# One shift of the SBUF layout: all operands of TensorE's products at equal addresses modulo 512 bytes

## The chip, the core and the metric

The kernel runs on one core of a Trainium2 chip. The metric is device time in microseconds of one execution. Three runs of the kernel before gave a median of 2284.33 us (2283.15 to 2285.94). The profile was taken in a separate execution.

## What is computed

One decoder block for a sequence of 2048 tokens with 1024 channels, all in float32. Cut to what matters here:

```python
h = rmsnorm(x, g_mix_pre) * (1.0 + scale_m) + shift_m       # scale, shift, gate from c @ w_cond
q, k, v, u = split(h @ w_in)                                # 8 heads of 64, and 512 pooling channels
z = einsum('bhqd,bhkd->bhqk', qb, kb) * inv_sqrt            # stick-breaking attention
log1m = where(mask, -softplus(z), 0.0)
after = cumsum(log1m, reverse=True) - log1m
w = where(mask, exp(log_sigmoid(z) + after), 0.0)
attn = einsum('bhqk,bhkd->bhqd', w, vb)
pool = pooling_mixer(u, w_pool, pool_scale)
x = x + gate_m * rmsnorm(concat([attn, pool]) @ w_out, g_mix_post)
h = rmsnorm(x, g_ffn_pre) * (1.0 + scale_f) + shift_f
f = (silu(h @ w_gate) * (h @ w_up)) @ w_down                # 1024 -> 2816 -> 1024
x = x + gate_f * rmsnorm(f, g_ffn_post)
```

## The kernel before

**Products.** Nearly every float32 operand is kept as a high part and a low part of type float32r, made by `split` (L55 to L60: a cast on ScalarE, a subtraction on VectorE or GpSimd). A product is then three matmuls, high by high, high by low and low by high (`mm3`, L64 to L71). `nc.tensor.matmul(ps, l, r)` loads `l` (128 columns, 512 bytes a partition) into the array and streams `r` (512 columns, 2048 bytes a partition) through it. In the profile the streamed operand stands first behind the arrow and the loaded one second: `b_g<-b22h,g_s_h` streams `b22h` past the loaded `g_s_h`. The load of the next matmul's operand (engine PEld) runs while the matmul before it streams.

**Stages**, by time from the start of the profiled execution:

| stage | us | what TensorE does |
|---|---|---|
| conditioning, first projections | 0 to 75 | sums for the modulation, transposes of the rows, first products |
| projections | 75 to 286 | q, k, u for the first half of the tokens (`pieces`), then v for all (`v_pieces`) |
| attention | 286 to 836 | per head and block: z (L828, L829), transposes of the weights (L863), values (L878, L879); between them q, k, u of the second half as filling (`pieces` again, L69 to L71) |
| output projection | 810 to 1008 | `mix_products`, transposes of the new rows (L125) |
| FFN, first half of the tokens | 1008 to 1646 | gate and up (to 1431), then down |
| FFN, second half | 1646 to 2284 | gate and up (to 2064), then down |

The FFN uses a seven-product scheme on half matrices. Its token operands `b11`, `b21`, `t2`, `t3`, `t1`, `t4`, `b22` are made by `new_ops` (L1046). In gate and up they are streamed, and a weight part made by `operand` (L1041) is loaded. In down, `add_block` (L1345) loads columns of the gated rows (`g0p`, `g1p`) and streams a part of `w_down` (`w0p`, `w1p`); both come from `operand`.

**Where tiles lie.** Pools stack up from the left end of a partition or down from the right end. A tile starts at a multiple of 32 bytes; a pool's tags follow each other in the order of their first use. The left side begins with `const` (`ident` at 128 modulo 512, `mhalf`, `sumsq`, `af`, `bf`), then `c1` (`ones`, `ones_r`, small columns), `wst`, `up`, and later `att`, `qk`, or `ring` and the FFN's operands, which follow directly behind `const`. Each `operand` pair has five buffers in `ring` on the left; every sixth call takes its pair from `fx` on the right instead (L1043). The `b22` of the first half lies on the right (`opsr`, L1644), that of the second half on the left (`ops1`, L1592). The addresses that the program gives to TensorE's operands, modulo 512 bytes:

| stage | streamed | loaded |
|---|---|---|
| q, k, u products | 480 | 480 (224 for the one chunk named `fourth`) |
| v products | 224 | 480 |
| z (L828, L829) | `kt` 128 | `qt` 128 |
| transposes of attention (L863) | `ident` 128 | `w` 384 |
| values (L878, L879) | `wth`, `wtl` 64 | `vt` 192 |
| output projection | 480 | 480 |
| FFN token operands and `ring` | 288 | 288 |
| `fx` pairs, and `b22` of the first half | 480 | 480 |
| conditioning (L571) | `wc` 224 | `cs` 160 to 184 |

So a `ring` weight at 288 meets the first half's `b22` at 480; an `fx` weight at 480 meets token operands at 288; and in down an `fx` part of `w_down` at 480 is streamed past gated rows at 288. The two `b22h` tiles lie at bytes 145376 (first half) and 144160 (second half), 1216 bytes apart.

**Order and waits.** Projections to attention, and the FFN, run in an order written out by hand on PE, ScalarE, VectorE and GpSimd (`manual_schedule`). A pool opened with `reuse_waits="tile"` lets a new tile wait for the old tiles whose bytes it takes. Attention's pools `att` and `qk` (L796, L797) take over bytes of the projections' `tok`, `wv` and `hc`.

Of the kernel before, what the change touches and what calls it, by code (L numbers as in the profile page):

```python
# [9 lines left out]
F32 = mybir.dt.float32  # L10
# [7 lines left out]
P = 128  # L18
# [10 lines left out]
TB = 512  # L29
# [4 lines left out]
OFF = 7  # L34
PRB = 6
# [9 lines left out]
def block_kernel(ctx, tc, x, c, w_cond, b_cond, g_mix_pre, g_mix_post, w_in, w_pool,  # L45
# [27 lines left out]
    def open_pool(stack, name, bufs=1, side=None):  # L73
        kw = {"side": side} if side else {}
        return stack.enter_context(tc.tile_pool(name=name, bufs=bufs, reuse_waits="tile", **kw))

    dram = ctx.enter_context(tc.tile_pool(name="dram", bufs=1, space=DRAM))
    const = ctx.enter_context(tc.tile_pool(name="const", bufs=1))
# [24 lines left out]
    mods = {n: const.tile([P, KC], F32, tag=n, name=n) for n in ("af", "bf")}  # L103
    mods["am"], mods["bm"] = sumsq[:, 0:KC], sumsq[:, KC:]

    fx = None

    def ft(tag, name, shape=(P, TB)):
# [33 lines left out]
    c1 = open_pool(ph1, "c1")  # L142
# [26 lines left out]
        nc.gpsimd.memset(rcnt[:, j:j + 1], 1.0 / (j + 1))  # L169
    colv = c1.tile([P, 68], F32, tag="colv", name="colv")  # L170
    cs = c1.tile([P, KC], F32, tag="cs", name="cs")
    halo = [c1.tile([P, 16], F32, tag=f"halo{g}", name=f"halo{g}") for g in range(NG)]

    hts = ExitStack()
# [3 lines left out]
    pro = ExitStack()  # L178
    hc = open_pool(pro, "hc", side="right")
    tokp = open_pool(pro, "tok", bufs=2, side="right")  # L180
    condst = ExitStack()
    cond = open_pool(condst, "cond", bufs=2, side="right")
    ht = {}
# [610 lines left out]


    att = open_pool(ph1, "att", bufs=2)  # L796
    qkp = open_pool(ph1, "qk", bufs=2)  # L797
    kv = {}

# [184 lines left out]
    for n in range(len(steps) + OFF):  # L984
# [4 lines left out]
        if n < len(steps):  # L989
            u, i = steps[n]  # L990
# [724 lines left out]
```

## Time and profile before

| | us |
|---|---|
| median of three runs | 2284.33 |
| the profiled execution's own time | 2285.23 |
| its span, first to last instruction | 2283.4 |
| PEld busy in it | 1847.4 |

The profile's page gives busy time by engine, the chain that ended last, and groups of instructions. TensorE's matmuls are pipelined, and their ends are modelled: a product that takes 0.39 us in a row of the trace overlaps its neighbours. What a product costs in a stream without waits is the distance from its start to the next one's start. Those distances are read from the timeline view, whose columns are start in us, duration in us, engine, source line, operation, out<-in, shapes and count; equal neighbours are merged into one row with their count.

### The profile page before, as it was taken

The page shows a single profiled execution, that of the slowest core. Times are in us where ns is not written, and L with a number is a line of the kernel's source. Part 1 is how long each engine was busy: PE and PEld are TensorE (multiplying, and loading weights), DVE is VectorE, ACT ScalarE, POOL GpSimd, SP SyncE. Part 2 cuts the span into 40 slices and gives each one's busy share as a digit, 9 for nine tenths or more (in the row PEclk, how much of TensorE's full clock was granted, in tenths as well). Part 3 has the DMA queues.
Part 4 walks back from the last instruction along what each step waited for, and adds up shares of the span by engine and source line. Part 5 has one row for each costly group of instructions (what it writes and reads, how often), then busy time and mean ns, then how long its engine had stood idle before and what let it go on. Part 6 is the DMA issues. An engine that isn't in the chain of part 4 may idle for free.

```text
span 2283.4 us, 33237 instructions
## 1 busy us (share of the span) xinstructions
PE 2247.0 (98%) x10605; PEld 1847.4 (81%) x10605; DVE 1619.5 (71%) x2212; ACT 1166.1 (51%) x2418; POOL 1295.7 (57%) x1607
## 2 busy tenths in 40 slices
PE   7999989999999999999999999999999999999998
PEld 5778878888888878887888888888888888888887
DVE  6774589999999966667656566786766565655566
ACT  4334579998899854443232323554533333334444
POOL 3552267787779965546777777331476565651003
PEclk9999999999999999999999999999999999999999
DMA  8885776634444356665545455776753332328654
GB/s 295 306 272 199 282 203 186 172 111 112 116 131 109 123 192 217 218 226 164 164 157 161 159 159 187 264 248 208 259 175 123 94 116 93 115 89 291 214 186 147
DMA packets 323979, 413.55 MB, mean 181 GB/s; under 512 B 20630, under 2 KB 189146, under 8 KB 323676
## 3 DMA queue, kind: packets, MB, share of 16 engines
q1 hardware_dynamic: 319484, 409.07, 55.7%
q10 hardware_dynamic: 4320, 2.36, 0.4%
q8 instruction: 83, 1.36, 0.2%
q14 instruction: 92, 0.75, 0.1%
HBM read 282.90 MB, written 128.45 MB: 180 GB/s over the span
## 4 chain that ended last, share of the span: by engine, by line
PE 90%; DVE 3%; ACT 2%; DMA 2%; POOL 2%; issue 1%; SPq 0%; DVEq 0%; POOLq 0%; ACTq 0%
PE wt L863 5%; PE t_g L69 3%; PE t_g L70 3%; PE t_u L70 3%; PE t_u L69 3%; PE t_u L71 3%; PE t_g L71 3%; PE dn0p L70 3%; PE dn0p L71 3%; PE dn0p L69 3%; PE dn1p L70 3%; PE dn1p L69 3%; PE dn1p L71 3%; PE b_u L70 3%; PE b_g L70 3%; PE b_g L69 3%
## 5 line engine op out<-in xcount | busy, mean ns | idle before, releaser
L852 POOL TENSOR_TENSOR w<-sg,pr 128x512 f32<-128x512 f32 (+2 forms) x320 | 306.7, 958 | 53.3 <-DVE pr L847 18.8
L1230 POOL TENSOR_TENSOR s<-s,cu 128x512 f32<-128x512 f32 x88 | 132.3, 1510 | 239.4 <-DVE cu L1229 146.5
L847 DVE TENSOR_TENSOR_SCAN pr<-pr,carry,begin 128x512 f32<-128x512 f32 x192 | 243.8, 1270 | 0.0
L831 ACT ACTIVATE sg<-z 128x512 f32<-128x512 f32 (+2 forms) x320 | 181.5, 567 | 54.4 <-PE z L829 44.3
L60 DVE TENSOR_TENSOR wtl<-wt,wth 128x512 fp32r<-128x512 f32 (+1 forms) x320 | 189.2, 591 | 19.9 <-ACT wth L59 18.2
L59 ACT CAST wth<-wt 128x512 fp32r<-128x512 f32 (+1 forms) x320 | 181.0, 567 | 11.9 <-PE wt L863 11.9
L833 ACT ACTIVATE pr<-z 128x512 f32<-128x512 f32 (+2 forms) x320 | 180.9, 565 | 0.0
L863 PE MATMUL wt<-ident,w 128*128 128x128 f32 x1088 | 172.2, 273 | 0.7 <-POOL pr L843 0.4
L60 DVE TENSOR_TENSOR u_s_l<-u_s,u_s_h 128x512 fp32r<-128x512 f32 x66 | 65.3, 989 | 145.9 <-ACT u_s_h L59 140.7
L863 PEld LDWEIGHTS wt<-ident,w 128*128 128x128 f32 x1088 | 134.0, 140 | 30.7 <-POOL pr L843 0.9
L1220 ACT ACTIVATE s<-s 128x512 f32<-128x512 f32 x88 | 55.7, 633 | 182.7 <-DVE s L1219 182.7
L878 PE MATMUL av<-wth,vt 128*128 128x512 f32 (+1 forms) x320 | 126.2, 394 | 1.7 <-ACT o L883 1.4
L828 PE MATMUL z<-kt,qt 128*128 128x512 f32 (+2 forms) x320 | 118.5, 370 | 6.6 <-DMA kt<-kd 5.1
L60 DVE TENSOR_TENSOR u_a_l<-u,u_a_h 128x512 fp32r<-128x512 f32 x66 | 73.0, 1108 | 71.0 <-ACT u_a_h L59 71.0
L70 PE MATMUL dn0p<-w0p_l,g0p_h 128*128 128x512 f32 x308 | 120.8, 392 | 0.6 <-DVE w0p_l L60 0.6
L69 PE MATMUL dn0p<-w0p_h,g0p_h 128*128 128x512 f32 x308 | 120.5, 391 | 0.0
L71 PE MATMUL dn0p<-w0p_h,g0p_l 128*128 128x512 f32 x308 | 120.3, 391 | 0.0
L879 PE MATMUL av<-wtl,vt 128*128 128x512 f32 (+1 forms) x320 | 117.6, 368 | 1.7 <-DVE wtl L60 1.4
L829 PE MATMUL z<-kt,qt 128*128 128x512 f32 (+2 forms) x320 | 117.1, 366 | 0.0
L844 DVE TENSOR_TENSOR_SCAN pr<-pr,zero,begin 128x128 f32<-128x128 f32 (+3 forms) x128 | 111.2, 870 | 7.0 <-ACT pr L833 6.6
L70 PE MATMUL dn1p<-w1p_l,g1p_h 128*128 128x512 f32 x292 | 114.4, 392 | 0.0
L69 PE MATMUL dn1p<-w1p_h,g1p_h 128*128 128x512 f32 x292 | 114.2, 391 | 0.0
(692 smaller groups left out, 7063.8 us busy)
## 6 DMA issues: line engine op xcount, KB each, us to landing
g<-in_w_gate_dram SPq DMA_DIRECT2D x42, 512.0 KB, 5.3
u<-in_w_up_dram SPq DMA_DIRECT2D x42, 512.0 KB, 4.1
wc<-in_w_cond_dram SPq DMA_DIRECT2D x32, 512.0 KB, 7.1
qt<-qd SPq DMA_DIRECT2D x64, 256.0 KB, 3.9
kt<-kd SPq DMA_DIRECT2D x96, 128.0 KB, 3.3
vt<-vd SPq DMA_DIRECT2D x48, 256.0 KB, 3.8
wd<-in_w_down_dram SPq DMA_DIRECT2D x44, 256.0 KB, 3.5
tdt<-wd SPq DMA_DIRECT2D x44, 256.0 KB, 2.0
```

Source lines behind the costliest of these rows:

```text
L59: nc.scalar.copy(hi, src)
L60: low.tensor_tensor(lo, src, raw(hi), ALU.subtract)
L69: nc.tensor.matmul(ps, lh, rh, start=first and i == 0, stop=False)
L70: nc.tensor.matmul(ps, lh, rl, start=False, stop=False)
L71: nc.tensor.matmul(ps, ll, rh, start=False, stop=last and i == n - 1)
L831: nc.scalar.activation(sg[:, 0:L], z[:, 0:L], AF.Sigmoid, scale=0.125)
L833: nc.scalar.activation(pr[:, 0:L], z[:, 0:L], AF.Sigmoid, scale=-0.125)
L847: nc.vector.tensor_tensor_scan(keys, keys, begin, carry, ALU.mult, ALU.bypass)
L852: nc.gpsimd.tensor_tensor(w[:, 0:L], sg[:, 0:L], pr[:, 1:L + 1], ALU.mult)
L863: nc.tensor.transpose(wt[:, i * P:(i + 1) * P], wss[u][i][:, b * P:(b + 1) * P], ident)
L878: nc.tensor.matmul(av[:, lo0:], vb, wh[:, lo0:], start=first, stop=False)
L1230: nc.gpsimd.tensor_tensor(s, s, u, ALU.mult)
```

## The change

A helper `lay_out` allocates tiles that nothing writes: one of each listed tag, which fixes the order of the tags in a pool, and one called `pad`. It is called four times.

```diff
+    def lay_out(pool, tags, pad):
+        for tag, bufs, words in tags:
+            pool.tile([P, words], F32, tag=tag, bufs=bufs, name=f"first_{tag}")
+        pool.tile([P, pad], F32, tag="pad", bufs=1, name="pad")
+
+    lay_out(const, (), 48)
...
     cs = c1.tile([P, KC], F32, tag="cs", name="cs")
+    lay_out(c1, (), 24)
...
     tokp = open_pool(pro, "tok", bufs=2, side="right")
+    lay_out(tokp, (("ss", 2, 1), ("rs_v", 2, 1), ("rs_r", 4, 1)), 64)
...
     att = open_pool(ph1, "att", bufs=2)
+    lay_out(att, (("vt", 6, TB), ("sg", 5, TB), ("w", OFF + 4, TB), ("wth", 4, TB), ("wtl", 4, TB), ("pr", PRB, TB + 1),
+                  *((f"carry{i}", 2, 1) for i in range(4))), 16)
```

No instruction is added, removed or put in another place on PE, ScalarE, VectorE, GpSimd or the DMA queue, apart from two semaphore waits on GpSimd. In the table above every operand of a product moves to 480 modulo 512, the conditioning's `cs` to 352 to 376; in the transposes `ident` stays at 128 and `w` moves from 384 to 480. `b22h` of the first half stays at byte 145376, that of the second half moves to 144352.

Since tiles lie elsewhere, some waits for old tiles move. At the start of attention the first tiles `pr` now wait for the last stores of v (`vd<-ve`), for which the first `wth` and `wtl` waited before; the first `w` no longer waits for a DMA. At the output projection the load of `gm` no longer waits for TensorE, and the first load of `xr` behind it waits for an earlier product than `gm` did.

## The prediction

> **What bounds the kernel now.** I read the page first, then TensorE's waits in the FFN, then stretches by stage.
>
> ```profile
> PE 2247.0 (98%) x10605; PEld 1847.4 (81%) x10605; DVE 1619.5 (71%) x2212; ACT 1166.1 (51%) x2418; POOL 1295.7 (57%) x1607
> ...
> PE 90%; DVE 3%; ACT 2%; DMA 2%; POOL 2%; issue 1%; SPq 0%; DVEq 0%; POOLq 0%; ACTq 0%
> ```
>
> ```profile
> PE t_g L69 <- DVE cu L1229: 1.2, 1, 1.2
> PE dn0p L70 <- DVE w0p_l L60: 0.6, 1, 0.6
> PE f_pt L125 <- DVE x1s L1095: 0.5, 1, 0.5
> ```
>
> ```profile
> 308.00:809.00 501.00, 496.78 (x2822) 417.57 (x2822) 487.03 (x631) 453.71 (x1034) 404.04 (x883) 1.00 0.50 142
> ...
> 1008.00:1431.00 423.00, 421.17 (x1850) 345.44 (x1849) 266.40 (x333) 136.69 (x246) 314.28 (x217) 1.00 0.53 171
> 1431.00:1646.00 215.00, 214.40 (x934) 174.87 (x934) 161.43 (x212) 113.59 (x213) 62.15 (x45) 1.00 0.73 241
> 1646.00:2064.00 418.00, 418.00 (x1842) 345.57 (x1842) 256.92 (x322) 133.34 (x235) 259.79 (x181) 1.00 0.38 118
> 2064.00:2266.00 202.00, 202.00 (x882) 165.11 (x881) 121.23 (x189) 96.00 (x184) 23.25 (x18) 1.00 0.65 219
> ```
>
> The chain that ended last is 90% TensorE. The three waits are all that TensorE has from 1008 to 2266 us: 2.3 us in 1258. The stretches (columns: length, then busy us of PE, PEld, DVE, ACT, POOL, the granted clock, the DMA share, GB/s) show the FFN filled by PE at full clock, with the next engine, POOL, at 314 of 423 us. A nanosecond off the spacing of a product there is a nanosecond off the end. Attention, 308 to 809 us, is different: DVE is busy 487 of 501 us, so what TensorE gains there may turn into waiting.
>
> **What an address costs.** No engine is idle inside the FFN's stream, so a slow product can only show as a longer distance between starts.
>
> ```profile
> 1965.27 0.39 PE L71 MATMUL t_g<-t4h,g_a_l 128*128 128x512 f32 x1
> ...
> 1979.09 0.39 PE L69 MATMUL t_u<-t1h,u_s_h 128*128 128x512 f32 x1
> ```
>
> ```profile
> 1660.35 0.39 PE L69 MATMUL b_g<-b22h,g_s_h 128*128 128x512 f32 x1
> ...
> 1662.84 0.39 PE L71 MATMUL b_g<-b22h,g_s_l 128*128 128x512 f32 x1
> ```
>
> ```profile
> 1037.03 0.39 PE L71 MATMUL b_g<-b22h,g_s_l 128*128 128x512 f32 x1
> ...
> 1038.43 0.39 PE L71 MATMUL b_g<-b22h,g_s_l 128*128 128x512 f32 x1
> ```
>
> From the first of these rows to the second lie 61 products, streamed and loaded operand both at 288: 13.82/61 = 226.6 ns each. The next two fences are the same product, b22 by the weight sum s4, in the two halves of the tokens. In the second half (both at 288) 11 distances make 2.49 us, 226 ns. In the first half (b22 at 480, weights at 288) 6 make 1.40 us, 233.3 ns. The two b22h tiles lie only 1216 bytes apart, and the weights use the same ring buffers, so neither the side of SBUF nor the kind of product separates them; the low address bits do. The other mixed classes of the FFN:
>
> ```profile
> 1439.32 0.39 PE L69 MATMUL dn0p<-w0p_h,g0p_h 128*128 128x512 f32 x1
> ...
> 1442.12 0.39 PE L69 MATMUL dn0p<-w0p_h,g0p_h 128*128 128x512 f32 x1
> ...
> 1443.50 0.39 PE L69 MATMUL dn0p<-w0p_h,g0p_h 128*128 128x512 f32 x1
> ```
>
> ```profile
> 1072.33 0.39 PE L69 MATMUL t_u<-t2h,u_s_h 128*128 128x512 f32 x1
> ...
> 1075.08 0.39 PE L69 MATMUL t_u<-t3h,u_s_h 128*128 128x512 f32 x1
> ```
>
> In down, twelve products that stream an fx tile (480) past rows at 288 take 2.80 us, 233.3 ns each. In gate and up, twelve that load an fx weight (480) under tokens at 288 take 2.75 us, 229.2 ns each. After the switch back to equal addresses at 1442.12 the first six distances still make 1.38 us where six at 226.6 make 1.36: a disturbance of 0.02 us that dies out.
> ```profile
> 853.60 0.39 PE L70 MATMUL mix<-wo_hblo,mh 128*128 128x512 f32 x1
> ...
> 861.99 0.39 PE L71 MATMUL mix<-wo_hahi,ml 128*128 128x512 f32 x1
> ```
>
> ```profile
> 207.95 0.39 PE L69 MATMUL v<-wvh,hth 128*128 128x512 f32 x1
> ...
> 209.31 0.60 PE L125 MATMUL x_pt<-ident,xs 128*128 128x128 f32 x4
> ```
>
> Equality at 480 is as good as at 288: 37 products of the output projection take 8.39 us, 226.8 ns each. So is v with 224 against 480, a distance of 256: six take 1.36 us. I count that class as already good and the projections as unchanged.
>
> One rule of the Trainium skill speaks against all this. In "TensorE: Matmul & The Clock Gate", section "Step-by-step: what each phase is for", streaming and weight loading have two independent read ports, and loading the next weights does not take SBUF bandwidth from the running matmul. By it, no address could matter and the sum below would be zero. The trace disagrees: 233.3 against 226.6 ns for one and the same product.
>
> **The change, part by part.** Paddings of const and thereby of ring and the FFN operands: streamed 480 past loaded 288 ends, and loaded 480 under streamed 288 ends.
> - Streamed 480, loaded 288: 19 blocks of b22 in the first half (22, less 3 whose weight lies in fx too) and every third chunk of down, 26 and 24 of them. Twelve products each: 69 x 12 = 828. Each falls from 233.3 to 226.6: 828 x 6.7 ns = 5.5 us.
> - Streamed 288, loaded 480: every sixth weight of gate and up, 22 blocks in the first half (25, less the same 3) and 26 in the second: 48 x 12 = 576. Each falls from 229.2 to 226.6: 1.5 us.
> - Switches between classes: 50 in down at 0.02 us, 1.0 us. Lower bound 0 (other disturbances may take their place), upper bound 2.0 with those of gate and up; I take 0.9.
>
> Together 7.9 us, all in the FFN, where PE alone sets the end. If another engine capped it, the next is POOL with 109 us of slack in the tightest stretch, so I deduct nothing.
>
> Attention: kt, qt, vt, wth, wtl and w move to 480. Here products come in short groups behind transposes, and a group never reaches the settled spacing.
>
> ```profile
> 484.76 0.48 PE L69 MATMUL u<-hth,wu_h 128*128 128x512 f32 x1
> 485.07 0.40 PE L70 MATMUL u<-htl,wu_h 128*128 128x512 f32 x1
> ...
> 486.45 0.60 PE L863 MATMUL wt<-ident,w 128*128 128x128 f32 x4
> ```
>
> ```profile
> 851.20 0.48 PE L69 MATMUL mix<-wo_hbhi,mh 128*128 128x512 f32 x1
> ...
> 851.75 0.40 PE L71 MATMUL mix<-wo_hbhi,ml 128*128 128x512 f32 x1
> 851.99 0.39 PE L69 MATMUL mix<-wo_hbhi,mh 128*128 128x512 f32 x1
> 852.21 0.39 PE L70 MATMUL mix<-wo_hblo,mh 128*128 128x512 f32 x1
> ...
> 852.91 0.40 PE L70 MATMUL mix<-wo_hblo,mh 128*128 128x512 f32 x1
> ```
>
> ```profile
> 482.02 0.48 PE L878 MATMUL av<-wth,vt 128*128 128x512 f32 x1
> ...
> 483.04 0.60 PE L863 MATMUL wt<-ident,w 128*128 128x128 f32 x4
> ```
>
> ```profile
> L828 PE MATMUL z<-kt,qt 128*128 128x512 f32 x224 | 89.3, 399 | 0.1
> ```
>
> A group of seven in attention takes 1.69 us from its first start to the next transposes. The nearest row for "all equal, just behind transposes" is the output projection: its first seven distances make 1.71 us. For the groups of four the pair is 1.02 and 1.01. So equal addresses do not help right behind transposes: +0.012 us (1.709 against 1.697 before rounding) for up to 192 groups with a filling (24 pieces of 8), nothing for the others. Upper bound +2.3 us; lower bound, if the groups do settle at 226.6, what attention's long products now lie above it. They are 4 x 224 of z and values (the row shows one of four lines) and 192 x 3 of the filling, 1470; from the second start of the group at 485.07, six make 1.38 us, 230 ns each, so 1470 x 3.4 ns = 5.0 us. I take +1.5, by the nearest row. The transposes stay load-bound: the order of PE is unchanged and `ident` does not move.
>
> Waits at attention's start. The first pr on ACT now waits for the last store of v:
>
> ```profile
> 287.88 0.34 SPq L496 DMA_DIRECT2D vd<-ve  x1
> ```
>
> ```profile
> DMA to landing us min/median/max: 2.9/3.1/4.3
> ```
>
> ```profile
> 292.50 0.27 ACT L833 ACTIVATE pr<-z 128x128 f32<-128x128 f32 x1
> ```
>
> 287.88 + 3.1 = 291.0 us, and even with 4.3 it is 292.2, ahead of 292.50: nothing. Queued behind that pr are ACT's next sigmoids, and PE behind their PSUM banks; without this cover each microsecond late would cost one. The gm load on SP is freed, not held. The other engines work by length, not address: the scans of pr, whose six buffers lie at six different offsets, all take the same time.
>
> ```profile
> L847 DVE TENSOR_TENSOR_SCAN pr<-pr,carry,begin x192: 1264/1270/1275, 303.9 to 814.4; 128x512 f32<-128x512 f32 x192
> ```
>
> The conditioning (L571) keeps unequal operands: 24 products, at most 7 ns each by the largest class difference seen, +-0.2 us; I take 0.
>
> **Sum.** -5.5 - 1.5 - 0.9 + 1.5 = -6.4 us against the profiled execution's own 2285.23 (span 2283.4 plus 1.8 around it): 2278.8. That execution lies 0.9 above the median of the runs, so against the median 2284.33 the forecast is 2277.9 us.
>
> **Rivals.**
> - Attention settles too (-5.0 in place of +1.5): 2271.4. For it: groups are short but regular. Against: the output projection needs about nine products behind transposes to settle, and DVE's 487 of 501 us would swallow part. Chance 0.08.
> - The addresses are not the cause, and the 6.7 ns move with something else: 2284.3. This is what that rule of the Trainium skill (TensorE: Matmul & The Clock Gate) would give. Against it stand the two b22 fences. Chance 0.09.
> - Slower: in attention all 1470 long products settle into the slowest distance seen at equal addresses behind transposes. In the output projection above, 851.75 to 851.99 is such a step, some 236 ns against 230 now: +8.8 us, in place of +1.5, gives 2284.33 - 7.9 + 8.8 = 2285.2. It decides from 7.9 us / 1470 = 5.4 ns per product. Against it: distances of 224 to 236 alternate there. Chance 0.08, with room above if the VectorE-bound pace of attention slips with it.
>
> **How the numbers follow.** The forecast has 0.70, with a range of its own from 2275.5 (switches 2.0, attention 0) to 2280 (switches 0, attention +2.3, and half a microsecond of noise). The remaining 0.05 is a half gain near 2281. Runs of before spread over 2.8 us, so about 0.2% (4.6 us, that is below 2279.8) is what a measurement can tell from no change. Faster by that: nearly all of the forecast and the first rival, 0.74. Within: the second rival, half gains and the near part of the third, 0.18. Slower: 0.08. The range for 8 in 10 takes in most of the first rival's way and the half gain: 2273 to 2281.5.
>
> **What would show it.** Right: b22 in the first half and the fx chunks of down at 226 to 227 ns like their neighbours; down's stretches shorter by about 2.5 us each; gate and up by about 2 and 1; attention's groups of seven at 1.70 to 1.72 us; the clock at 1.00. Wrong: b22 of the first half still at 233; or attention longer by more than 3 us; or a new wait of ACT or PE between 290 and 300 us.

## The result, and the profile after

The kernel with the change takes 2277.66 us (median of 8 runs, 2276.41 to 2279.36), the kernel before on the same chip 2283.97 (8 runs, 2282.96 to 2285.94). The ratio is 0.9969, with a 95% interval of 0.996 to 0.9978: a gain of 0.3%. The profiled execution of after took 2279.36 us with a span of 2277.6.

The page of after, first the busy times, then the chain that ended last:

```profile
PE 2240.0 (98%) x10605; PEld 1848.5 (81%) x10605; DVE 1630.1 (72%) x2212; ACT 1165.6 (51%) x2418; POOL 1292.6 (57%) x1607
...
PE 88%; DVE 3%; DMA 3%; ACT 2%; POOL 2%; issue 1%; SPq 0%; DVEq 0%; POOLq 0%; ACTq 0%
```

TensorE issues the same 10605 matmuls and is busy 7.0 us less (2247.0 before). The others stay within 11 us of before. The same five stretches as before (length, then busy us and instructions of PE, PEld, DVE, ACT, POOL, the granted clock, the DMA share, GB/s):

```profile
308.00:809.00 501.00, 496.78 (x2823) 416.95 (x2821) 486.12 (x629) 452.77 (x1031) 402.85 (x879) 1.00 0.50 141
1008.00:1431.00 423.00, 421.16 (x1864) 347.94 (x1863) 268.68 (x335) 136.79 (x247) 314.91 (x218) 1.00 0.53 172
1431.00:1646.00 215.00, 214.12 (x945) 176.91 (x945) 165.76 (x214) 114.62 (x214) 64.31 (x46) 1.00 0.73 244
1646.00:2064.00 418.00, 417.66 (x1842) 345.28 (x1842) 259.00 (x325) 132.62 (x234) 259.50 (x182) 1.00 0.38 119
2064.00:2266.00 202.00, 202.00 (x893) 167.33 (x892) 122.52 (x191) 97.35 (x187) 25.02 (x22) 1.00 0.65 218
```

Where an engine is full both before and after, busy time says nothing, but the count does: the last down stretch passes 893 products in its 202 us where it passed 882, and 11 x 0.227 = 2.5 us. The first gate and up has 14 more (3.2 us), the first down 11 more. The second gate and up, 1646 to 2064 us, has none more, and its busy time fell from 418.00 to 417.66: TensorE idled there, which it did not before.

The two places of the FFN that the prediction named, in the timeline of after, are the first half's `b22` and a chunk of down whose `w0p` lies in `fx`:

```profile
1037.78 0.39 PE L69 MATMUL b_g<-b22h,g_s_h 128*128 128x512 f32 x1
...
1038.92 0.39 PE L71 MATMUL b_g<-b22h,g_s_l 128*128 128x512 f32 x1
```

```profile
1437.62 0.39 PE L69 MATMUL dn0p<-w0p_h,g0p_h 128*128 128x512 f32 x1
...
1440.34 0.39 PE L69 MATMUL dn0p<-w0p_h,g0p_h 128*128 128x512 f32 x1
```

Five distances make 1.14 us, 228 ns by rows rounded to 0.01 (233.3 before); twelve make 2.72 us, 226.7 ns (233.3 before).

The next table cuts each profiled span at the first product of each stage (us; "rest" is everything else). The kernels named e_... are the experiments below.

| kernel | attention | gate, up 1 | down 1 | gate, up 2 | down 2 | rest |
|---|---|---|---|---|---|---|
| before | 517.96 | 426.37 | 212.94 | 419.57 | 211.61 | 494.9 |
| after | 519.45 | 423.50 | 210.62 | 419.83 | 209.21 | 495.0 |
| e_const | 520.97 | 423.56 | 210.63 | 418.88 | 209.21 | 493.3 |
| e_256 | 519.46 | 423.55 | 210.62 | 419.74 | 209.21 | 492.4 |
| e_att | 519.44 | 426.38 | 212.93 | 419.57 | 211.61 | 494.8 |
| e_32 | 520.04 | 434.27 | 209.55 | 431.20 | 209.28 | 493.6 |
| e_ffn | 518.75 | 423.57 | 210.62 | 419.09 | 209.21 | 493.6 |
| e_ident | 519.39 | 423.67 | 210.62 | 418.88 | 209.21 | 494.4 |
| e_best | 519.00 | 423.53 | 210.63 | 418.88 | 209.21 | 494.2 |
| e_again | 521.46 | 423.52 | 210.62 | 419.81 | 209.21 | 494.2 |

From before to after the FFN gives 2.87 + 2.32 - 0.26 + 2.40 = 7.33 us; attention takes 1.49 back. Single profiles of one program differ by 2 us in attention (after and e_again are the same program), by 0.1 us or less in the FFN: so the FFN's columns can be compared by themselves, attention's only together with the rows of the trace behind them.

**The second gate and up.** TensorE's waits of after from 1005 to 2270 us are the three of before and a fourth (columns: who waits, for whom, us in total, times, longest). One of the three, in the first down, has grown from 0.6 to 0.9 us. The grown one and the fourth:

```profile
PE dn0p L70 <- DVE w0p_l L60: 0.9, 1, 0.9
...
PE b_g L69 <- ACT dn0p L1449: 0.2, 1, 0.2
```

The timeline shows the fourth as two long steps, 0.63 and 0.49 us in place of 0.23:

```profile
1656.17 0.39 PE L71 MATMUL t_g<-t4h,g_a_l 128*128 128x512 f32 x1
1656.80 0.50 PE L69 MATMUL b_g<-b22h,g_s_h 128*128 128x512 f32 x1 [0.24 <-ACT dn0p L1449]
...
1659.43 0.39 PE L71 MATMUL b_g<-b22h,g_s_l 128*128 128x512 f32 x1
1659.92 0.50 PE L69 MATMUL b_u<-b11h,u_a_h 128*128 128x512 f32 x1
```

The products want PSUM banks in which the first half's last `dn0p` rows still stand; ScalarE's square (L1449) must read them first. Both steps together cost 0.40 + 0.27 us, and the steps after them take some 0.2 us to settle again. That square is late because of a chain that starts on POOL, goes on through ScalarE and VectorE (each instruction of it released by the one before, or behind it on its engine) and ends in the square. Here it is in after, with the issue of the transfer that POOL waits for at the top and the square at the end, and then in e_ident, which has the same FFN addresses and no such wait:

```profile
1626.99 0.37 ACTq L1161 DMA_DIRECT2D g<-in_w_gate_dram  x1
...
1639.12 1.29 POOL L1166 TENSOR_TENSOR g_s<-g 128x512 f32<-128x512 f32 x1 [4.18 <-DMA cr<-f0d]
...
1641.74 0.55 POOL L1471 TENSOR_TENSOR sumsq<-sumsq,mhalf 128x1 f32<-128x1 f32 x1
...
1642.32 0.73 ACT L1494 ACTIVATE y_v<-y_v,sumsq 128x512 f32<-128x512 f32 x1 [6.52 <-POOL sumsq L1471]
...
1656.04 0.58 ACT L1449 ACTIVATE dn0p<-y_u 128x512 f32<-128x512 f32 x1
```

```profile
1637.16 1.28 POOL L1167 TENSOR_TENSOR g_s<-g 128x512 f32<-128x512 f32 x1 [2.77 <-DMA g<-in_w_gate_dram]
...
1639.76 0.55 POOL L1472 TENSOR_TENSOR sumsq<-sumsq,mhalf 128x1 f32<-128x1 f32 x1
...
1654.09 0.58 ACT L1450 ACTIVATE dn0p<-y_u 128x512 f32<-128x512 f32 x1
```

In e_ident TensorE stands 0.54 us earlier, but POOL and the square 1.96 and 1.95 us: in after everything behind POOL's wait for a transfer runs 1.4 us later against TensorE. The transfer is that of the gate weights `g`, which POOL's instruction reads: in all seven profiles with equal FFN addresses it lands 0.13 us ahead of that instruction, and the row names it in six (after's names another that landed with it). It is issued 12.7 to 13.3 us ahead of the stage's first product, but from issue to landing it takes 12.0 us in after (12.1 in e_again, 12.0 in e_256), 11.4 in e_ffn, and 10.5 to 10.6 in e_ident, e_best and e_const (10.2 in before). POOL's wait and the stage go together in all seven: 4.18, 4.15 and 4.07 us of waiting (after, e_again, e_256) with stages of 419.83, 419.81 and 419.74; 3.43 (e_ffn) with 419.09; 2.77, 2.79 and 3.01 (e_ident, e_best, e_const) with 418.88 each.

**Attention.** A group with a filling, four transposes and seven products, in after, and TensorE's clock at the start of attention in before, after and e_again:

```profile
485.66 0.60 PE L874 MATMUL wt<-ident,w 128*128 128x128 f32 x4
486.01 0.48 PE L69 MATMUL u<-hth,wu_h 128*128 128x512 f32 x1
...
487.72 0.60 PE L874 MATMUL wt<-ident,w 128*128 128x128 f32 x4
```

```profile
292.00:297.00 5.00, 5.00 (x19) 4.01 (x18) 1.61 (x3) 2.40 (x8) 1.13 (x4) 0.69 0.88 195
```

```profile
292.00:297.00 5.00, 5.00 (x14) 4.24 (x15) 1.23 (x2) 1.71 (x6) 1.19 (x4) 0.50 0.96 205
```

```profile
292.00:297.00 5.00, 4.56 (x17) 3.53 (x16) 2.12 (x3) 2.80 (x9) 1.19 (x4) 0.75 0.82 179
```

The seven take 1.71 us as predicted. Over the 75 full groups of eleven (four transposes and seven products of 512 columns) the median distance from transposes to transposes is 2051 to 2054 ns before and 2060 after, for q, k and u alike. Take every step between starts from the first z to 809 us that begins with a product of 512 columns: what lies a little (under 14 ns) above the settled 226.7 ns sums to 5.23 us before and 6.20 after (6.26 in e_again). So about 1.0 us is the cost of the new addresses. Some half a microsecond more goes with the clock: behind the 5 us wait for `kt` it was granted at 0.69 before and 0.50 after (the column behind the five engines), and the first twenty products took 6.18 and 6.64 us. In e_again, the same program as after, the clock is 0.75 and they take 6.12, so this half is not fixed by the layout.

### The profile page after: what moved, and what is told of

Read it like the earlier page. It is cut to its first block, busy times and chain, and to the rows that moved or that the text cites. A ratio compares the mean times of both kernels' runs of the same rounds, so it can differ in the third digit from the quotient of the medians.

```text
span 2277.6 us, 33239 instructions
## 1 busy us (share of the span) xinstructions
PE 2240.0 (98%) x10605; PEld 1848.5 (81%) x10605; DVE 1630.1 (72%) x2212; ACT 1165.6 (51%) x2418; POOL 1292.6 (57%) x1607
## 4 chain that ended last, share of the span: by engine, by line
PE 88%; DVE 3%; DMA 3%; ACT 2%; POOL 2%; issue 1%; SPq 0%; DVEq 0%; POOLq 0%; ACTq 0%
PE wt L874 5%; PE t_u L71 3%; PE t_u L69 3%; PE t_u L70 3%; PE t_g L69 3%; PE t_g L70 3%; PE t_g L71 3%; PE dn0p L70 3%; PE dn0p L71 3%; PE dn0p L69 3%; PE dn1p L70 3%; PE dn1p L69 3%; PE dn1p L71 3%; PE b_u L69 3%; PE b_u L71 3%; PE b_u L70 3%
## 5 line engine op out<-in xcount | busy, mean ns | idle before, releaser
L59 ACT CAST g_s_h<-g_s 128x512 fp32r<-128x512 f32 x66 | 39.5, 621 | 150.6 <-POOL g_s L1173 80.6
L59 ACT CAST u_s_h<-u_s 128x512 fp32r<-128x512 f32 x66 | 38.6, 613 | 151.0 <-POOL u_s L1173 149.3
```

Of the source, the lines that this page charges most:

```text
L59: nc.scalar.copy(hi, src)
```

## The experiments

**probe: what a distance between addresses costs.** Behind the last product of after, series of 28 float32r products with one streamed operand and one loaded operand, each series with the loaded one 32 bytes further:

```diff
...
+    def series(name, at, off, cols=P, count=28):
+        ps = f_ps(name)
+        for i in range(count):
+            nc.tensor.matmul(ps[0:cols], loaded[:, at:at + cols], moving[:, off:off + TB], start=i == 0, stop=i == count - 1)
+
+    for n in range(16):
+        series(f"pr_d{n}", 8 * n, 0)
+    for n in (2, 6, 10, 14):
+        series(f"pr_e{n}", 8 * n, 64)
+    for cols in (64, 32):
+        series(f"pr_c{cols}", 0, 0, cols)
```

> The kernel after, with series of products added behind its last one: 28 matmuls each, 128 columns loaded and 512 streamed, the streamed tile fixed at 480 modulo 512 and the loaded one 32 bytes further in each of 16 series; four series repeat with the streamed tile 256 bytes further; two load only 64 and 32 columns. The output is untouched; the time is not to be compared. Theory (spacing depends on the distance modulo 256): distance 0 and 256 give 226.6 ns, 64 and 320 (the class of the first half's b22) both 233.3, 192 and 448 (the class of an fx weight) both about 229. Rival (modulo 512): 320 gives 233.3 and 192 gives 229, but 64, 256 and 448 give values of their own. Second rival (the skill's independent ports, the classes differ for another reason): all 16 series at one spacing. On size: if the load takes SBUF time from the stream, 64 and 32 columns fall to about 220 and 217 ns; if the 226.6 is a fixed cost of a product, they stay at 226.6.

Measured: 2423.87 us in all. The timeline of the probe merges equal products, and the windows asked for cut the series, so a row counts fewer than 28; a merged row's length less the last product's 0.39 us, over its count less one, is the step. At a distance of 256 bytes, of 320, of 192, and then at 0 with 64 loaded columns:

```profile
2332.73 3.79 PE L1711 MATMUL pr_d<-probe_moving,probe_loaded 128*128 128x512 f32 x16
```

```profile
2345.68 3.90 PE L1711 MATMUL pr_d<-probe_moving,probe_loaded 128*128 128x512 f32 x16
```

```profile
2319.81 3.83 PE L1711 MATMUL pr_d<-probe_moving,probe_loaded 128*128 128x512 f32 x16
```

```profile
2409.70 4.53 PE L1711 MATMUL pr_c<-probe_moving,probe_loaded 128*64 128x512 f32 x19
```

These are 226.7, 234.0, 229.3 and 230.0 ns. Over the last twenty steps of each series the map by distance (loaded less streamed, modulo 512) is:

```
  0: 226.7   32: 233.3   64: 233.3   96: 234.3  128: 232.4  160: 233.2  192: 229.1  224: 233.3
256: 226.7  288: 233.3  320: 233.3  352: 234.3  384: 232.4  416: 233.1  448: 229.1  480: 233.3
```

(The series at 0 began at half the clock; its value is that of its last steps.) The map repeats after 256 bytes, to 0.1 ns, and with the streamed operand at 224 in place of 480 the four distances tried again give the same. 320 (before's loaded `ring` under a streamed 480) and 192 (a loaded `fx` under 288) are the 233.3 and 229.2 of the prediction. Only distance 0 modulo 256 reaches 226.7. What was expected of fewer loaded columns failed on both sides: 64 columns take 229.7 and 32 take 231.6, slower than 128.

**e_const: the first padding alone.** Of the change only the 48 words behind `const`; attention's operands on the left move along and keep their distances from each other.

```diff
+    lay_out(const, (), 48)
```

> The padding of const alone: FFN operands move to 480 as in the change; attention's operands keep their mutual distances of before. Theory (the FFN gains 6 to 8 us from equal addresses; attention lost 1.5 us by being made equal): FFN stretches as after, attention back at 518.0 us from the first z to the first mix product (before 518.0, after 519.5), time about 2276.2 us. Rival (attention's 1.5 us is chance or comes from the moved waits, not from equal addresses): attention at 518 to 520 in no relation to it, time as after, 2277.7.

Measured 2277.51 us (6 runs; before 2284.4), ratio 0.9967 [0.9955, 0.9979]: all of the gain, within what can be told. Attention takes 520.97 us, above the 518.0 of the theory and the 518 to 520 of the rival. Its groups are longer than after's, 2071 ns in the median (probe2 below gives this layout 2067 by itself), and its profile has a step in attention that after's does not have. That step shows a second price of a wait, in the timeline and the stretch behind it:

```profile
381.16 0.50 PE L885 MATMUL av<-wth,vt 128*128 128x512 f32 x1 [1.78 <-ACT o L890]
...
382.07 0.62 PE L835 MATMUL z<-kt,qt 128*128 128x512 f32 x1
382.50 0.63 PE L836 MATMUL z<-kt,qt 128*128 128x512 f32 x1
```

```profile
382.00:385.00 3.00, 3.00 (x11) 2.47 (x10) 2.33 (x5) 2.44 (x6) 1.36 (x3) 0.51 0.51 115
```

1.78 us of waiting are followed by 3 us at half the clock, with steps of 0.43 us. e_again, which is after's program, has the same step at 382.76 with 2.14 us. These two are the longest attention stages of the table. But a wait of that length need not cost this: in e_ident the same product waits as long, and the clock stays full.

```profile
382.86 0.50 PE L890 MATMUL av<-wth,vt 128*128 128x512 f32 x1 [1.79 <-ACT o L895]
```

```profile
383.00:386.00 3.00, 3.00 (x19) 2.64 (x20) 2.19 (x4) 3.00 (x9) 1.12 (x4) 1.00 0.45 98
```

The last section comes back to the difference.

**e_256: equal modulo 256 only.** The first padding with 112 words: the FFN's left side comes to 224, so the products that mixed left and right now lie 256 apart. The other three paddings are left out.

```diff
-    lay_out(const, (), 48)
+    lay_out(const, (), 112)
```

> const padded by 112 words instead: ring and FFN operands lie at 224, the fx pairs and the first half's b22 at 480, so every mixed product of the FFN is 256 bytes off modulo 512. Attention keeps its distances of before. Theory (modulo 256 decides): spacing 226.6 in all of the FFN, time as with const padded by 48, about 2276.2. Rival (modulo 512 decides): the mixed products stay near 229 to 233, time 2281 to 2284.

Measured 2278.24 us (6 runs), ratio 0.997 [0.9958, 0.9981]; the FFN's stages are after's to 0.1 us. Modulo 256 is what counts.

**e_att: attention's part alone.** No padding behind `const`, 72 words behind `c1`, `tok` and `att` as in the change: attention equal, the FFN as before.

```diff
+    lay_out(c1, (), 72)
...
+    lay_out(tokp, (("ss", 2, 1), ("rs_v", 2, 1), ("rs_r", 4, 1)), 64)
...
+    lay_out(att, (("vt", 6, TB), ("sg", 5, TB), ("w", OFF + 4, TB), ("wth", 4, TB), ("wtl", 4, TB), ("pr", PRB, TB + 1),
+                  *((f"carry{i}", 2, 1) for i in range(4))), 16)
```

> No padding of const, all the rest of the change: attention's products equal at 480, FFN as before (288 against 480). Theory: FFN as before, attention 1.5 us longer, time about 2285.5. Rival (attention's equal addresses gain as well, and the 1.5 us came from elsewhere): at or under 2284.

Measured 2285.88 us (11 runs; before 2284.4), ratio 1.0007 [0.9998, 1.0016]. The FFN is before's to 0.01 us, its last down stretch back at before's count:

```profile
2064.00:2266.00 202.00, 202.00 (x882) 165.13 (x881) 120.67 (x188) 95.19 (x180) 24.12 (x19) 1.00 0.66 218
```

Attention has groups of 2060 ns and is 1.48 us longer. This half of the change gives nothing and, by the groups, loses; the interval of the whole time just includes no change.

**e_32: the opposite.** After, with 32 bytes of padding behind `ring`'s buffers. The token operands on the left lie 32 bytes further, at 0, while the weights stay at 480, so the 3432 products of gate and up that stream them have a distance of 480, which is 224 modulo 256. Down's products keep theirs.

```diff
     ring = open_pool(ctx, "ring", bufs=RB)
+    lay_out(ring, (("wh", RB, TB), ("wl", RB, TB), ("w32", 1, 2 * KC * P)), 8)
```

> The kernel after, with 32 bytes of padding behind the ring: the FFN's token operands on the left now lie at 0 modulo 512 and the weights that are loaded under them at 480; down and all other stages stay equal. 3432 products of gate and up get a distance of 224 modulo 256, whose series on the chip took 233.3 ns against 226.7. Theory (the distance alone sets the spacing): 3432 x 6.6 ns = 22.7 us more, about 2300.3 us, all of it in the two gate and up stretches. Rival (only the gross layout, right against left, mattered): 2277.7.

Measured 2300.23 us (4 runs), 22.6 above after; 3432 x 6.6 ns = 22.7 was expected. Ratio to before 1.0069 [1.0053, 1.0084].

```profile
1040.04 0.40 PE L69 MATMUL t_u<-t1h,u_s_h 128*128 128x512 f32 x1
...
1042.61 0.40 PE L71 MATMUL t_u<-t1h,u_s_l 128*128 128x512 f32 x1
```

Eleven distances make 2.57 us, 233.6 ns. Down, whose addresses are after's, is 1.07 us shorter in the first half, where its one wait of 0.9 us is gone, and the same to 0.1 us in the second. One shift of 32 bytes with the same instructions costs three and a half times what the change gains: addresses are the cause, and the prediction's second rival falls. The Trainium skill ("TensorE: Matmul & The Clock Gate", section "Step-by-step: what each phase is for") has the two read ports independent, and a load takes no read bandwidth from the running product; by that no address should matter, and this run disagrees by 6.7 ns for each product. Which of the two reads loses the time no run here separates.

**e_ffn: the FFN's part alone.** The 48 words behind `const`, and 80 behind `c1`, which bring attention back to before's addresses modulo 512.

```diff
+    lay_out(const, (), 48)
...
+    lay_out(c1, (), 80)
```

> Padding of const by 48 words for the FFN, and of c1 by 80 words, so that attention lies 512 bytes further in all: each of its operands has the address of before modulo 512. Theory (attention's groups of 11 matmuls, 2.053 us before and 2.060 after, are set by addresses): 2.053 us again, FFN as after, time 2276.4. Rival (the longer groups come from the moved waits or from chance): 2.06 us, time as after, 2277.7.

Measured 2277.25 us (6 runs), ratio 0.9967 [0.9956, 0.9979]. Attention's groups are back at 2053 ns and the sum above the settled step at 5.25 us (after 6.20): that 1.0 us is the addresses. The total is 0.4 us under after's, which runs of this spread can't tell apart.

**e_ident: the identity too.** After, with 88 words ahead of `ident`, so that the transposes' streamed operand comes to 480 as well.

```diff
+    const.tile([P, 88], F32, tag="before_ident", name="before_ident")
     ident = const.tile([P, P], F32, tag="ident", name="ident")
...
-    lay_out(const, (), 48)
+    lay_out(const, (), 88)
```

> The kernel after, with ident moved to 480 too, so that the transposes' streamed and loaded operands are equal as well. Theory (the unequal transposes disturb the products behind them): groups of 11 at 2.05 us or less, attention 1 us shorter or more, time about 2276.5. Rival (the switch from transposes to products disturbs whatever the addresses): groups stay at 2.06, time as after, 2277.7.

Measured 2277.61 us (6 runs), ratio 0.9969 [0.9958, 0.9981]. The groups' median stays at 2060 ns: the rival was right. Transposes follow each other after 108.7 ns on average in every kernel, whatever the address of `ident`. The second gate and up has four products more than after's in its stretch, and TensorE full:

```profile
1646.00:2064.00 418.00, 418.00 (x1846) 346.12 (x1845) 255.68 (x324) 132.28 (x234) 260.13 (x182) 1.00 0.38 119
```

**probe2: groups of eleven by themselves.** Behind the last product, attention's group (four transposes, three products of a filling, two of values, two of z) twelve times for each layout of its operands.

```diff
...
+    group("pr_before", 128, 128, 224, 224, 192, 64, 128, 128)
+    group("pr_after", 128, 224, 224, 224, 224, 224, 224, 224)
+    group("pr_const", 128, 64, 224, 224, 128, 0, 64, 64)
+    group("pr_equal", 224, 224, 224, 224, 224, 224, 224, 224)
+    group("pr_beforei", 224, 128, 224, 224, 192, 64, 128, 128)
```

(The arguments are the addresses modulo 256 of the identity, the transposed tile, the filling's streamed and loaded operand, the values' loaded and streamed one, and z's two; 14 further layouts varied single ones.)

> The kernel after, with copies of attention's group of 11 (4 transposes, 3 products of the filling, 2 of the values, 2 of z) behind its last product, 12 of each layout; the output is untouched, the time is not to be compared. Theory (addresses set the group): the layout of before gives 2.053 us, that of after 2.060, that of the kernel with const padded alone 2.064 to 2.072, and a layout exists under 2.05. Rival (semaphores and waits in the real attention set the differences): all layouts give the same within 2 ns.

Measured: 2748.25 us in all; per group, medians of 2058 ns for before's layout, 2060 for after's, 2067 for e_const's, 2060 for all equal, 2047 for before's with the identity at 224; the other layouts lie between 2053 and 2076. Before's layout came out 5 ns above what was expected, after's and e_const's as expected, and one lies under 2050; the rival, all layouts alike, falls. Two stretches of the timeline, after's layout and "before, identity moved":

```profile
2316.47 0.60 PE L1717 MATMUL pr_aftert<-ident,probe_plain 128*128 128x128 f32 x4
2316.83 1.87 PE L1719 MATMUL pr_after<-probe_moving,probe_loaded 128*128 128x512 f32 x7
2318.53 0.60 PE L1717 MATMUL pr_aftert<-ident,probe_plain 128*128 128x128 f32 x4
```

```profile
2392.67 0.60 PE L1717 MATMUL pr_beforeit<-probe_ident,probe_plain 128*128 128x128 f32 x4
2393.02 1.85 PE L1719 MATMUL pr_beforei<-probe_moving,probe_loaded 128*128 128x512 f32 x7
2394.72 0.60 PE L1717 MATMUL pr_beforeit<-probe_ident,probe_plain 128*128 128x128 f32 x4
```

2.06 and 2.05 us. A group with all operands equal is not the fastest, and no layout reaches the settled step: the six steps behind the first product average 231.5 ns in after's layout, and at 226.7 they would make a group of 2031. Right behind transposes, equality buys nothing.

**e_best and e_again: the best of these, and the change once more.** e_best is e_ffn with the identity moved as in e_ident; e_again is after.

> The FFN's paddings, attention's operands at the low addresses of before, and the identity of the transposes moved to the streamed operands' address (modulo 256). Theory (short groups are set by the addresses inside a group, as in the group probe, where this layout made 2047 ns against 2058 with the identity where before has it): the groups of eleven with a filling fall from 2053 ns to about 2047 or less, 192 of them, 1.2 to 2.1 us below e_ffn: 2275.1 to 2276.1 us. Rival (moving the identity gave nothing in e_ident, so it gives nothing here): groups at 2053 ns and 2277.3 us.

> The change once more, on the same chip as e_best, for the comparison: 2277.7 us, with the 0.5 and 0.6 us waits at 1656 and 1659 us again in the second gate and up, so that stage at 419.8 us; the rival, that these waits are chance, has the stage at 418.9.

Measured on one chip: e_best 2277.37 us (5 runs), ratio 0.9964 [0.9951, 0.9976]; e_again 2278.31 (6 runs), ratio 0.9967 [0.9955, 0.9979]. The probe's 2047 ns did not carry over: in e_best the groups with k take 2047 ns, those with u 2067 and with q 2062, and the sum above the settled step is 5.76 us against e_ffn's 5.25. The rival of e_best was right. e_again has the two long steps at 1657 us again and 419.81 us in that stage, and its stretch has after's count:

```profile
1646.00:2064.00 418.00, 417.71 (x1842) 345.36 (x1841) 259.60 (x324) 132.59 (x235) 259.61 (x182) 1.00 0.38 119
```

So both profiles of this layout have the wait. That does not yet rule chance out: every other program was profiled once, and of those with equal FFN addresses e_256 has a stage just as long, e_ffn one of 419.09, and three have none of it. No version beats the change by more than can be measured.

## Why the prediction was right, and where it was not

The forecast was 2277.9 us and the median is 2277.66. The parts agree a little less well than that: by the two profiles the kernel gained 5.9 us where the sum had 6.4, and after's profile lies 1.7 us above its own median. That the total is met to 0.3 us is in part luck.

- **Mixed products and switches in the FFN, 7.9 us.** Measured 7.33. The mechanism is shown both ways (e_ffn alone has the gain, e_32 alone the loss). The parts can be measured by putting the program's addresses to each of the 5544 products of the FFN in the trace, in order. (A step of more than 40 ns above 226.6 counts as a wait.) In before, the products at distance 64 lie 6.7 ns above 226.6, and their sum is 1.54 us in the first gate and up and 2.10 and 1.94 in the two downs: 5.6 us, where the prediction had 5.5. Those at distance 192 sum to 0.82 and 0.74 us: 1.6, where it had 1.5. The products at equal addresses in the first gate and up and the two downs lie 0.52, 0.50 and 0.46 us further above 226.6 in before than in after: 1.5 us for the disturbance at the switches, where it had 0.9. These gains come to 8.6 us. Against them stand waits, counted at nothing: the one of the first down that grew, 0.28 us, and those of the next point, 1.0 us.
- **"I deduct nothing" failed in one place above all.** The second gate and up should have gained 26 x 12 x 2.6 ns = 0.8 us and lost 0.26. The step that failed is the reading of a stretch's mean: POOL had 109 us of slack over the tightest stretch, yet stood 4.2 us before one transfer, and the chain behind it frees a PSUM bank some 17 us on (in before it stood 2.3 us at that place). The transfer took 12.0 us in place of 10.2, and TensorE ran into the end of the chain. Where it took 10.5 to 10.6 us the stage takes 418.88, 0.69 less than before, near the forecast. That the transfer is the cause is read from the order of the rows and seven profiles; it wasn't tried by moving the transfer, and why it takes longer in some of them is open.
- **Attention, +1.5 us.** Measured +1.49 in this profile, but its parts differ: about 1.0 us from the groups (7 ns in the median and 4 in the mean of the full ones, for the 12 taken from one pair of rows) and about 0.5 from the clock at attention's start, which e_again, the same program, does not have. The forecast's size was luck; its sign was right, and so was the choice of the nearest row (short stretches behind transposes) over the settled step.
- **Rivals.** "Attention settles too" falls by probe2 and e_att; "the addresses are not the cause" by e_32 and e_const; "slower, all long products at 236 ns" by the groups of 2060 ns.
- **What was counted at nothing**: the new waits of `pr` at the start of attention do not show among TensorE's waits, as argued; the projections and the conditioning moved by less than the profiles differ among themselves (the "rest" column spans 2.6 us).
- **Modulo 512 or 256.** The prediction counted 224 against 480 as already good from one row of the v products. probe and e_256 make it a rule of this chip's runs.

## What to carry to other kernels

In a stream of back-to-back products of one size, read the step between starts by operand pair; if the same product has two steps, compare the operands' addresses before looking for a wait. Lay out loaded and streamed operands at the same address modulo 256 bytes where products come in long runs (here 2.5 to 6.7 ns in 227 for each), and leave short groups behind transposes alone. A gain on the engine that sets the end moves it against all the others: look for single late transfers behind a stage's start, which no mean over the stage shows.

## What the runs showed of the hardware that was not expected

- The step of a product depends on the distance of its two operands modulo 256 with a pattern that is not monotonic (192: 229.1, 224: 233.3, 0: 226.7), and loading half or a quarter of the columns makes it longer (229.7, 231.6).
- The granted clock changes on a grid. In each of the twelve profiles all its changes lie whole multiples of 3.413 us apart; at attention's start it is half from 291.68 to 295.10 us in before and from 291.28 to 298.11 in after, one interval and two. At the wait near 382 us, what counts is how much of it falls into one interval: 1.77 (probe2), 1.78 (e_const) and 2.14 us (e_again) within one were each followed by 3.41 us at half the clock, while the 1.79 us of e_ident (1.46 and 0.32) and the 1.85 of e_32 (0.86 and 0.99), cut in two by the grid, and all the shorter waits left it at 1.00. This is read from twelve profiles; no run moved a wait against the grid on purpose. The Trainium skill ("TensorE: Matmul & The Clock Gate", section "What's actually happening") puts an idle window at about 3.4 us; the interval agrees, but about half of one without a product sufficed here. Its half rate agrees: a granted clock of 0.51 and steps of 0.43 us.
- One load of the same gate weights, issued at the same point of the schedule, took 10.2 to 12.1 us to land in ten profiles of kernels that differ only in where tiles lie and in a few waits.
